# w_up of a hybrid decoder layer in three 256-column matmuls a tile, with stationary weights at bytes 64 and 192 of a line

## The chip, the cores and the metric

The kernel runs on one core of a Trainium2 chip. The metric is the device time of one execution in microseconds (us). TensorE (PE) does the matmuls; its weight loads (PEld) are instructions of their own. VectorE (DVE), ScalarE (ACT) and GpSimd (POOL) do the rest, and SyncE (SP) issues most transfers.

## The reference

One layer, 256 tokens, width 2048, all float32: an RMS norm, one input projection, sliding-window attention beside a Mamba-2 state-space part, an output projection, and then the part that the change is about, a feed-forward network with a causal convolution over three tokens:

```python
def _conv_ffn(hn, w_up, ffn_conv_w, ffn_conv_b, w_down):
    u = _causal_dwconv(hn @ w_up, ffn_conv_w, ffn_conv_b)
    gate, val = u[..., :D_FF], u[..., D_FF:]
    return (jax.nn.silu(gate) * val) @ w_down
```

D_FF is 5632, so w_up is 2048 x 11264 and w_down 5632 x 2048.

## The kernel before, in words

Every matmul operand is split in two float32r parts, `hi` (a rounded copy, made by ScalarE) and `lo` (the rest, a VectorE subtraction). A product a x b is taken as hi x hi + hi x lo + lo x hi, accumulated in PSUM. Weights come from HBM in blocks of 1 MB (512 input rows x 512 columns, as 128 partitions x 2048) into a tile `raw` (three buffers), and `pieces` and `split` (lines 75 to 101) turn each half into a `hi` and a `lo` tile of 128 x 1024 (four buffers each).

There are two kinds of product. `gemm_tok` (line 186) keeps the activations stationary and streams 512 columns of weights; it serves the q, z, k, v, w_out and (by its own loop) w_down parts. `gemm_chan` (line 212) keeps a 128 x 128 piece of the weights stationary and streams the activations of all 256 tokens, so that its output has channels on partitions, as the convolutions want it. It serves two places:

- the x, B and C channels of the state-space part: eight calls, two in each of four stretches, with `wide=False`. A tile (one 128-row block of input by 128 output channels) takes three matmuls of 256 columns: lines 229 (`hi` with the activations' `hi`), 230 (`hi` with their `lo`) and 231 (`lo` with their `hi`).
- w_up: 22 calls with `wide=True`. A tile takes two matmuls. Since the two parts of the activations of one block lie one behind the other, line 237 streams both, 512 columns, past `hi` into a whole PSUM bank; line 235 streams the 256 of `hi` past `lo` into the bank's first half. `conv` (line 243) then adds the halves, with a copy on ScalarE (line 247) and an add on VectorE (line 248), before it applies the norm's factor (249) and the taps (252, 254).

A call goes through 4 blocks x 4 output tiles x 4 input rows of 128: 64 tiles. Calls for the gate half write the four PSUM banks `acc`, those for the value half the four banks `aux`, in turn.

Where tiles begin in SBUF is set by hand. Weight and activation tiles are aligned to a line of 256 bytes, and an offset in bytes is added: `W_AT` = 0 for the weights of `gemm_tok` and of w_up, `C_AT` = 64 for those of the x/B/C calls, `X_AT` = 0 for the activations of all parts but w_up, and `H_AT` = 32 for w_up's (`h2T`). All pieces inside a tile are multiples of 256 bytes, so each matmul's operand keeps its tile's offset.

The order on each engine is made when the kernel is built, by a scheduler that models times. Small jobs (transposes, attention, state-space steps) are put between the matmuls of a large product by `later` and `step` (lines 176 to 184); in w_up only the first call has any: eight transposes (line 159) and four matmuls that spread the norm's factor (line 141).

Of the kernel before, what the change touches and what calls it, by code (L numbers as in the profile page):

```python
# [11 lines left out]
F32R = mybir.dt.float32r  # L12
I32 = mybir.dt.int32
AF = mybir.ActivationFunctionType
ALU = mybir.AluOpType
# [4 lines left out]
P = 128  # L20
D = 2048
S = 256
NT = S // P
NKT = D // P
# [14 lines left out]
HALF = 1024  # L39
LINE = 256  # L40

W_AT, C_AT, X_AT, H_AT = 0, 64, 0, 32

PAR_MIX, PAR_ATT, PAR_SSD, PAR_FFN = 0, 16, 32, 48
PAR_CW, PAR_CB = 64, 192
# [7 lines left out]
def hymba(ctx, tc, x, xt, w_kd, w_in, w_out, w_up, w_down, par, vecs, gfin, con, out):  # L53
# [20 lines left out]

    def split(raw, o, n, at):
        hi, lo = (
            wp.tile([P, HALF + C_AT // 4], F32R, tag=t, name=t, bufs=4, align_bytes=LINE)[:, at // 4 : at // 4 + n]
            for t in ("hi", "lo")
        )
        A.copy(out=hi, in_=raw[:, o : o + n])  # L80
        V.tensor_tensor(out=lo, in0=raw[:, o : o + n], in1=hi.bitcast(F32), op=ALU.subtract)  # L81
        return hi, lo

    def pieces(src, width, parts, load=None, work=None, at=W_AT):

        n = width // parts
        per = RAWW // n
        raws = [wp.tile([P, RAWW], F32, tag="raw", name="raw", bufs=3) for _ in range(-(-parts // per))]
        part = lambda h: raws[h // per][:, h % per * n : (h % per + 1) * n]
        if load:  # L90
            for h in range(parts):
                load(h)
                SY.dma_start(out=part(h), in_=src[:, h * n : (h + 1) * n])
        else:
            SY.dma_start(out=raws[0][:, :width], in_=src)
        out = []
        for h in range(parts):
            if work:
                work(h)
            out.append(split(part(h), 0, n, at))  # L100
        return out

    def acts(pool, at, **kw):
        return placed(pool, NKT * 2 * S, at, **kw).rearrange("p (k i s) -> p k i s", i=2, s=S)
# [10 lines left out]
    def col(base, i):  # L115
        c = base + i
        return parn_t[:, c : c + 1] if c < NNORM else parc_t[:, c - NNORM : c - NNORM + 1]
# [49 lines left out]
    def mm3(o, lh, ll, rh, rl, first, last):  # L167
        PE.matmul(out=o, lhsT=lh, rhs=rh, start=first, stop=False)  # L168
        PE.matmul(out=o, lhsT=lh, rhs=rl, start=False, stop=False)  # L169
        PE.matmul(out=o, lhsT=ll, rhs=rh, start=False, stop=last)  # L170
# [38 lines left out]
                if i < nb - 1 or m < 3:  # L209
                    step()  # L210

    def gemm_chan(blocks, actT, evac, tag="acc", wide=True):

        b = [acc(tag) for _ in range(4)]
        nb = len(blocks)
        for i, src in enumerate(blocks):
            got = pieces(src, 2048, 2, at=W_AT if wide else C_AT)
            last = i == nb - 1
            for ks in [(0, 1, 2, 3)] if last else [(0, 1), (2, 3)]:
                for ct in range(4):  # L220
                    for k in ks:
                        hi, lo = got[k // 2]
                        kt = 4 * i + k
                        o = (k % 2) * 512 + ct * P
                        end = kt == NKT - 1
                        rh = actT[:, kt, 0, :]
                        wh, wl = hi[:, o : o + P], lo[:, o : o + P]
                        if not wide:
                            PE.matmul(out=b[ct][:, :S], lhsT=wh, rhs=rh, start=kt == 0, stop=False)  # L229
                            PE.matmul(out=b[ct][:, :S], lhsT=wh, rhs=actT[:, kt, 1, :], start=False, stop=False)  # L230
                            PE.matmul(out=b[ct][:, :S], lhsT=wl, rhs=rh, start=False, stop=end)  # L231
                            continue
                        for lo_turn in (True, False) if end else (False, True):
                            if lo_turn:
                                PE.matmul(out=b[ct][:, :S], lhsT=wl, rhs=rh, start=False, stop=False)  # L235
                            else:
                                PE.matmul(out=b[ct], lhsT=wh, rhs=actT[:, kt, :, :], start=kt == 0, stop=end)  # L237
                    if last:
                        evac(ct, b[ct])
                    if (ct < 3) if last else (ct % 2):  # L240
                        step()

    def conv(dst, b, rB, wcol, bias, taps, wide):

        u = up.tile([P, S], F32, tag="cu", name="cu", bufs=3)
        if wide:
            A.copy(out=u, in_=b[:, S:])
            V.tensor_tensor(out=u, in0=b[:, :S], in1=u, op=ALU.add)
            V.tensor_tensor(out=u, in0=u, in1=rB, op=ALU.mult)
        else:  # L250
            V.tensor_tensor(out=u, in0=b[:, :S], in1=rB, op=ALU.mult)
        A.activation(out=dst, in_=u, func=AF.Identity, scale=wcol(taps - 1), bias=bias)
        for j in range(1, taps):
            V.scalar_tensor_tensor(  # L254
                out=dst[:, j:], in0=u[:, : S - j], scalar=wcol(taps - 1 - j), in1=dst[:, j:],
                op0=ALU.mult, op1=ALU.add,
            )
# [517 lines left out]
    for zi in range(4):  # L775
        es, parts, zt = {}, {}, {}

        def z_load(zi=zi, zt=zt):
            zt[0] = sp.tile([P, NT, 512], F32, tag="zs", name="zs", bufs=1)
            G.dma_start(out=zt[0].rearrange("p t d -> p (t d)"), in_=z_d[zi])  # L780

        def decay_loads(zi=zi, es=es):
            for g in (2 * zi, 2 * zi + 1):
                es[g] = decay_load(g)

        for g in (2 * zi, 2 * zi + 1):
            u = up.tile([P, 4, S], F32, tag="u", name="u", bufs=2)

            def evac_u(ct, b, u=u, g=g, zt=zt):
                cidx = 2 * g + ct if ct < 2 else (16 + g if ct == 2 else 24 + g)  # L790
                conv(u[:, ct, :], b, r1B, lambda k: col(PAR_CW + 32 * k, cidx), col(PAR_CB, cidx), 4, False)
                A.activation(out=u[:, ct, :], in_=u[:, ct, :], func=AF.Silu)
                if g % 2 and ct == 3:
                    A.activation(out=zt[0], in_=zt[0], func=AF.Silu)

            def part(i, g=g, u=u, es=es, parts=parts):
                if i == 0:
                    parts[g] = ssd(g, es, u)
                parts[g][i]()

            gemm_chan([w_in[5 + 3 * zi + g % 2, i] for i in range(4)], xT, evac_u, wide=False)
            if g % 2 == 0:
                later((1 if zi else 11, decay_loads), (4 if zi else 14, z_load))
            later(*(
                (off, f) for off, f in zip(
                    (5, 7, 11, 13) if g % 2 else (4, 6, 10, 12) if zi else (13, 14, 18, 20),
                    (
                        lambda g=g, es=es: decay(g, es[g]), lambda part=part: part(0),
                        lambda part=part: part(1), lambda part=part: part(2),
                    ),  # L810
                )
            ))

        def gates(zi=zi, parts=parts, zt=zt):
            for g in (2 * zi, 2 * zi + 1):
                parts[g][3](zt[0])

        gemm_att(zi)
        later(
            (1, gates), (7, lambda zi=zi, parts=parts: parts[2 * zi][4]()),  # L820
            (9, lambda zi=zi, parts=parts: parts[2 * zi + 1][4]()), *(((10, open_hp),) if zi == 3 else ()),
        )

    h2T = acts(cp, H_AT, tag="xT", name="h2T")
    ss2 = cp.tile([P, NT, 4], F32, name="ss2")
    s2 = cp.tile([P, NT], F32, name="s2")
    r2 = cp.tile([P, NT], F32, name="r2")
# [25 lines left out]
    for c in range(11):  # L853
        gate = up.tile([P, 4, S], F32, tag="u", name="gate", bufs=2)

        def evac_f(ct, b, val, c=c, gate=gate):
            i = 4 * c + ct
            ci = i + (NFT if val else 0)
            if val:
                dst = fp.tile([P, S], F32, tag="cv", name="cv", bufs=3)  # L860
            else:
                dst = gate[:, ct, :]
            conv(dst, b, r2B, lambda k: col(PAR_FW + 88 * k, ci), col(PAR_FB, ci), 3, True)
            if val:
                G.tensor_tensor(out=gT[:, i, :], in0=gate[:, ct, :], in1=dst, op=ALU.mult)  # L865
            else:
                A.activation(out=dst, in_=dst, func=AF.Silu)

        for val in range(2):
            gemm_chan(  # L870
                [w_up[2 * c + val, i] for i in range(4)], h2T, lambda ct, b, val=val: evac_f(ct, b, val),
                tag="aux" if val else "acc",
            )
# [164 lines left out]
```

## Time and profile before

| | |
|---|---|
| median of three runs | 1402.37 us (1401.41 to 1402.73) |
| profiled execution | 1398.48 us, span 1396.8 |
| PE busy | 1379.1 us, 99% of the span |
| DVE, ACT, POOL busy | 985.3, 796.0, 174.8 us |
| mean granted TensorE clock | 0.997 of full speed |
| moved by DMA | 271.76 MB, 195 GB/s |

The span is the profiled execution from the first to the last instruction. A matmul's printed duration includes a modelled end that lies beside the next matmul; when matmuls follow each other closely, the distance from start to start is what one costs. Some matmul records can be missing, so distances are taken over several rows. Times in the timeline are counted from the start of the span. By stage: the q, k, v and z parts with attention up to 258.8 us, the x/B/C stretches alternating with parts of w_out from there to 567, the rest of w_out to 657.8, w_up to 1148.2, w_down to 1387.3, and the final norm.

### The profile page before, as it was taken

To read this page: it belongs to the slowest core of one execution; us is meant where nothing else is said; L and a number is where in the kernel's file an instruction comes from. 1 tells how busy PE (TensorE), PEld (TensorE's weight loads), DVE (VectorE), ACT (ScalarE), POOL (GpSimd) and SP (SyncE) were. 2 spreads that over 40 slices of the span, in tenths; PEclk is the share of its full clock that TensorE was granted. 3 is DMA by queue.
4 is the path that set the end of the run, shared out by engine and by line. 5 is a ranking of instruction groups with operands and counts; after the bars stand their busy time and mean duration, and the time that the engine had idled before them with its cause. 6 is when DMAs were issued, how large, how long until landed. Compare 5 with 4: busy or idle time off the path is not lost.

```text
span 1396.8 us, 20383 instructions
## 1 busy us (share of the span) xinstructions
PE 1379.1 (99%) x7797; PEld 1209.5 (87%) x7797; DVE 985.3 (71%) x1488; ACT 796.0 (57%) x1275; POOL 174.8 (13%) x162
## 2 busy tenths in 40 slices
PE   8999999999999999999999999999999999999997
PEld 8888888998989899888888888888888888888886
DVE  6668788888777777655686867777687775555555
ACT  6567777775656564544564555546555554444444
POOL 0002112223111212100011101110011100000001
PEclk9999999999999999999999999999999999999999
DMA  9754544556556464656555555555555555555552
GB/s 306 263 182 166 196 151 172 190 182 209 209 187 240 170 238 169 239 185 220 191 188 184 189 201 182 181 198 179 196 193 199 181 181 209 182 200 192 187 204 91
DMA packets 44594, 271.76 MB, mean 195 GB/s; under 512 B 5056, under 2 KB 7232, under 8 KB 14672
## 3 DMA queue, kind: packets, MB, share of 16 engines
q1 hardware_dynamic: 40288, 254.69, 51.3%
q0 software_dynamic: 4208, 15.76, 3.7%
q8 instruction: 61, 1.00, 0.3%
q14 instruction: 37, 0.30, 0.1%
HBM read 264.11 MB, written 6.32 MB: 194 GB/s over the span
## 4 chain that ended last, share of the span: by engine, by line
PE 90%; DVE 3%; DMA 2%; ACT 2%; issue 1%; POOL 0%; SPq 0%; DVEq 0%; POOLq 0%; ACTq 0%
PE acc L237 11%; PE aux L237 11%; PE acc L168 11%; PE acc L170 11%; PE acc L169 11%; PE aux L235 6%; PE acc L235 6%; PE acc L231 3%; PE acc L230 3%; PE acc L229 3%; PE aux L169 3%; PE aux L170 3%; PE aux L168 3%; DVE lo L81 1%; PE aux L686 1%
## 5 line engine op out<-in xcount | busy, mean ns | idle before, releaser
L81 DVE TENSOR_TENSOR lo<-raw,hi 128x1024 fp32r<-128x1024 f32 (+1 forms) x480 | 586.3, 1229 | 328.3 <-ACT hi L80 326.7
L80 ACT CAST hi<-raw 128x1024 fp32r<-128x1024 f32 (+1 forms) x480 | 491.8, 1033 | 403.3 <-PE aux L170 126.6
L237 PE MATMUL acc<-h2T,hi 128*128 128x512 f32 x704 | 243.4, 391 | 0.0
L237 PE MATMUL aux<-h2T,hi 128*128 128x512 f32 x704 | 243.0, 391 | 0.0
L235 PE MATMUL aux<-h2T,lo 128*128 128x256 f32 x704 | 191.1, 282 | 0.0
L235 PE MATMUL acc<-h2T,lo 128*128 128x256 f32 x704 | 191.0, 282 | 0.0
L237 PEld LDWEIGHTS aux<-h2T,hi 128*128 128x128 f32 x704 | 129.8, 188 | 24.6
L237 PEld LDWEIGHTS acc<-h2T,hi 128*128 128x128 f32 x704 | 129.8, 188 | 24.5
L229 PE MATMUL acc<-xT,hi 128*128 128x256 f32 x512 | 143.8, 283 | 0.0
L230 PE MATMUL acc<-xT,hi 128*128 128x256 f32 x512 | 143.5, 282 | 0.0
L231 PE MATMUL acc<-xT,lo 128*128 128x256 f32 x512 | 141.5, 280 | 1.9 <-DVE lo L81 1.9
L235 PEld LDWEIGHTS acc<-h2T,lo 128*128 128x128 f32 x704 | 132.9, 189 | 3.9
L235 PEld LDWEIGHTS aux<-h2T,lo 128*128 128x128 f32 x704 | 132.9, 189 | 3.8
L168 PE MATMUL acc<-hi,xT 128*128 128x512 f32 (+2 forms) x320 | 113.9, 375 | 5.9 <-ACT hi L80 5.9
L170 PE MATMUL acc<-hi,xT 128*128 128x512 f32 (+2 forms) x320 | 118.6, 374 | 0.0
L169 PE MATMUL acc<-lo,xT 128*128 128x512 f32 (+2 forms) x320 | 118.5, 374 | 0.0
L865 POOL TENSOR_TENSOR gT<-gate,cv 128x256 f32<-128x256 f32 x44 | 61.1, 1390 | 434.6 <-DVE cv L254 424.1
L231 PEld LDWEIGHTS acc<-xT,lo 128*128 128x128 f32 x512 | 96.5, 190 | 2.5 <-DVE lo L81 2.1
L230 PEld LDWEIGHTS acc<-xT,hi 128*128 128x128 f32 x512 | 97.1, 190 | 0.6
L229 PEld LDWEIGHTS acc<-xT,hi 128*128 128x128 f32 x512 | 96.5, 189 | 0.3
L168 PEld LDWEIGHTS acc<-hi,xT 128*128 128x128 f32 x320 | 59.3, 191 | 15.0 <-ACT hi L80 5.9
L169 PEld LDWEIGHTS acc<-lo,xT 128*128 128x128 f32 x320 | 61.1, 191 | 9.2
(225 smaller groups left out, 2278.0 us busy)
## 6 DMA issues: line engine op xcount, KB each, us to landing
raw<-in_w_up SPq DMA_DIRECT2D x88, 1024.0 KB, 4.8
raw<-in_w_in SPq DMA_DIRECT2D x68, 1024.0 KB, 4.8
raw<-in_w_down SPq DMA_DIRECT2D x44, 1024.0 KB, 4.8
raw<-in_w_out SPq DMA_DIRECT2D x32, 1024.0 KB, 4.9
raw<-in_w_kd SPq DMA_DIRECT2D x16, 272.0 KB, 4.9
e<-acs_d POOLq DMA_DIRECT2D x8, 512.0 KB, 6.6
xraw<-in_xt SPq DMA_DIRECT2D x16, 128.0 KB, 4.4
x_r<-in_x SPq DMA_DIRECT2D x2, 1024.0 KB, 6.0
```

The source lines that it names most:

```text
L80: A.copy(out=hi, in_=raw[:, o : o + n])
L81: V.tensor_tensor(out=lo, in0=raw[:, o : o + n], in1=hi.bitcast(F32), op=ALU.subtract)
L168: PE.matmul(out=o, lhsT=lh, rhs=rh, start=first, stop=False)
L169: PE.matmul(out=o, lhsT=lh, rhs=rl, start=False, stop=False)
L170: PE.matmul(out=o, lhsT=ll, rhs=rh, start=False, stop=last)
L229: PE.matmul(out=b[ct][:, :S], lhsT=wh, rhs=rh, start=kt == 0, stop=False)
L230: PE.matmul(out=b[ct][:, :S], lhsT=wh, rhs=actT[:, kt, 1, :], start=False, stop=False)
L231: PE.matmul(out=b[ct][:, :S], lhsT=wl, rhs=rh, start=False, stop=end)
L235: PE.matmul(out=b[ct][:, :S], lhsT=wl, rhs=rh, start=False, stop=False)
L237: PE.matmul(out=b[ct], lhsT=wh, rhs=actT[:, kt, :, :], start=kt == 0, stop=end)
L686: PE.matmul(out=b[:, o : o + HD], lhsT=e[:, c, h, :], rhs=xc[:, c, h, :], start=True, stop=True)
L865: G.tensor_tensor(out=gT[:, i, :], in0=gate[:, ct, :], in1=dst, op=ALU.mult)
```

## The change

w_up loses its own form: `gemm_chan` has one path, the three 256-column matmuls of `mm3`, for both of its places, and `conv` loses the copy and the add of the wide form. `split` takes one offset for `hi` and one for `lo`: weights of `gemm_tok` and w_down stay at 0, those of `gemm_chan` now lie at 64 (`hi`) and 192 (`lo`). `h2T` goes from offset 32 to 0. For the x/B/C calls the one difference is that `lo` lies at 192 and not at 64.

```diff
-W_AT, C_AT, X_AT, H_AT = 0, 64, 0, 32
+W_AT, C_AT, X_AT = (0, 0), (64, 192), 0
...
         hi, lo = (
-            wp.tile([P, HALF + C_AT // 4], F32R, tag=t, name=t, bufs=4, align_bytes=LINE)[:, at // 4 : at // 4 + n]
-            for t in ("hi", "lo")
+            wp.tile([P, HALF + most // 4], F32R, tag=t, name=t, bufs=4, align_bytes=LINE)[:, a // 4 : a // 4 + n]
+            for t, a, most in zip(("hi", "lo"), at, C_AT)
         )
...
-            got = pieces(src, 2048, 2, at=W_AT if wide else C_AT)
+            got = pieces(src, 2048, 2, at=C_AT)
...
-                        for lo_turn in (True, False) if end else (False, True):
-                            if lo_turn:
-                                PE.matmul(out=b[ct][:, :S], lhsT=wl, rhs=rh, start=False, stop=False)
-                            else:
-                                PE.matmul(out=b[ct], lhsT=wh, rhs=actT[:, kt, :, :], start=kt == 0, stop=end)
+                        mm3(
+                            b[ct][:, :S], hi[:, o : o + P], lo[:, o : o + P], actT[:, kt, 0, :], actT[:, kt, 1, :],
+                            kt == 0, kt == NKT - 1,
+                        )
...
-        if wide:
-            A.copy(out=u, in_=b[:, S:])
-            V.tensor_tensor(out=u, in0=b[:, :S], in1=u, op=ALU.add)
-            V.tensor_tensor(out=u, in0=u, in1=rB, op=ALU.mult)
-        else:
-            V.tensor_tensor(out=u, in0=b[:, :S], in1=rB, op=ALU.mult)
+        V.tensor_tensor(out=u, in0=b[:, :S], in1=rB, op=ALU.mult)
...
-    h2T = acts(cp, H_AT, tag="xT", name="h2T")
+    h2T = acts(cp, X_AT, tag="xT", name="h2T")
```

On PE, where the last part of w_out (activations `yT`) ends and w_up (`h2T`) begins, there stands before:

```order
L168 MATMUL acc<-hi,yT 128x512
L169 MATMUL acc<-lo,yT 128x512
L170 MATMUL acc<-hi,yT 128x512
L237 MATMUL acc<-h2T,hi 128x512
L235 MATMUL acc<-h2T,lo 128x256
```

and now (the lines of `mm3` are numbered one higher):

```order
L169 MATMUL acc<-hi,yT 128x512
L170 MATMUL acc<-lo,yT 128x512
L171 MATMUL acc<-hi,yT 128x512
L169 MATMUL acc<-h2T,hi 128x256
L170 MATMUL acc<-h2T,hi 128x256
L171 MATMUL acc<-h2T,lo 128x256
```

Up to this place every engine has the same instructions in the same order in both kernels; from here on two matmuls a tile have become three. On VectorE, at the end of the first w_up call of the value half (`aux` is the PSUM bank, `cu` the convolution's input, `cv` its output, `lo` a piece of the next weights), before:

```order
L249 TENSOR_TENSOR cu<-cu,r2B 128x256
L254 SCALAR_TENSOR_TENSOR cv<-cu,parc_t,cv 128x255
L248 TENSOR_TENSOR cu<-aux,cu 128x256
L254 SCALAR_TENSOR_TENSOR cv<-cu,parc_t,cv 128x254
L254 SCALAR_TENSOR_TENSOR cv<-cu,parc_t,cv 128x255
L249 TENSOR_TENSOR cu<-cu,r2B 128x256
L254 SCALAR_TENSOR_TENSOR cv<-cu,parc_t,cv 128x254
L81 TENSOR_TENSOR lo<-raw,hi 128x1024 x2
```

and now:

```order
L238 TENSOR_TENSOR cu<-aux,r2B 128x256 x2
L241 SCALAR_TENSOR_TENSOR cv<-cu,parc_t,cv 128x255 x2
L241 SCALAR_TENSOR_TENSOR cv<-cu,parc_t,cv 128x254
L238 TENSOR_TENSOR cu<-aux,r2B 128x256
L241 SCALAR_TENSOR_TENSOR cv<-cu,parc_t,cv 128x254
L238 TENSOR_TENSOR cu<-aux,r2B 128x256
L82 TENSOR_TENSOR lo<-raw,hi 128x1024
```

The add is gone, the multiplication reads PSUM itself, and the pieces of the next weights stand among the taps in another order.

## Rows read from the trace of the kernel before

**Rows 1.** The page: busy us (share of span) and count; granted clock in 40 slices.

```profile
PE 1379.1 (99%) x7797; PEld 1209.5 (87%) x7797; DVE 985.3 (71%) x1488; ACT 796.0 (57%) x1275; POOL 174.8 (13%) x162
...
PEclk9999999999999999999999999999999999999999
```

**Rows 2.** Windows by stage: us; PE, PEld, DVE, ACT, POOL busy (count); clock, DMA.

```profile
258.85:314.45 55.60, 53.74 (x438) 53.00 (x437) 49.44 (x95) 42.21 (x83) 12.99 (x13) 0.97 0.57 190
343.32:392.11 48.79, 48.79 (x423) 48.68 (x421) 38.11 (x64) 29.73 (x43) 9.33 (x10) 1.00 0.66 238
...
491.82:541.39 49.57, 49.43 (x425) 49.10 (x423) 36.87 (x67) 29.36 (x45) 11.32 (x11) 1.00 0.61 213
...
657.78:1148.15 490.37, 490.37 (x2829) 433.50 (x2828) 361.86 (x533) 271.73 (x404) 57.67 (x42) 1.00 0.54 191
1148.15:1387.30 239.15, 239.15 (x1057) 198.01 (x1055) 129.40 (x146) 108.13 (x143) 9.26 (x9) 1.00 0.50 178
```

**Rows 3.** Groups by line, w_up on PE: busy us, mean ns, idle before.

```profile
L237 PE MATMUL acc<-h2T,hi 128*128 128x512 f32 x704 | 243.4, 391 | 0.0
...
L235 PE MATMUL acc<-h2T,lo 128*128 128x256 f32 x704 | 191.0, 282 | 0.0
```

**Rows 4.** Timeline of PE, one w_up call: start us, us, what.

```profile
703.62 0.40 PE L237 MATMUL acc<-h2T,hi 128*128 128x512 f32 x1
703.85 0.28 PE L235 MATMUL acc<-h2T,lo 128*128 128x256 f32 x1
...
725.85 0.40 PE L237 MATMUL aux<-h2T,hi 128*128 128x512 f32 x1
```

**Rows 5.** Timeline of PE, second x/B/C stretch, middle part.

```profile
353.21 0.60 PE L159 MATMUL aux<-con_t,y 128*128 128x128 f32 x4
...
365.01 0.28 PE L229 MATMUL acc<-xT,hi 128*128 128x256 f32 x1
...
366.03 0.28 PE L229 MATMUL acc<-xT,hi 128*128 128x256 f32 x1
...
381.80 0.59 PE L676 MATMUL aux<-xw,b 128*128 128x256 f32 x2
```

**Rows 6.** Timeline of PE, the same stretch, its beginning and end.

```profile
343.09 0.39 PE L170 MATMUL acc<-hi,attT 128*128 128x512 f32 x1
343.32 0.28 PE L229 MATMUL acc<-xT,hi 128*128 128x256 f32 x1
...
344.02 0.28 PE L229 MATMUL acc<-xT,hi 128*128 128x256 f32 x1
...
382.46 0.28 PE L229 MATMUL acc<-xT,hi 128*128 128x256 f32 x1
...
383.52 0.28 PE L229 MATMUL acc<-xT,hi 128*128 128x256 f32 x1
...
391.99 0.28 PE L231 MATMUL acc<-xT,lo 128*128 128x256 f32 x1
```

**Rows 7.** Waits: us, times, longest; the last row from 258 to 310, others w_up.

```profile
DVE lo L81 <- ACT hi L80: 119.0, 89, 2.6
ACT hi L80 <- PE acc L237: 83.2, 59, 3.3
...
PE acc L231 <- DVE lo L81: 1.9, 1, 1.9
```

**Rows 8.** Timeline of PE, the last job of another kind in w_up.

```profile
671.64 0.38 PE L141 MATMUL aux<-diag,ones 128*128 128x128 f32 x2
```

**Rows 9.** Groups by line: what `conv` and the split of the weights take.

```profile
L81 DVE TENSOR_TENSOR lo<-raw,hi 128x1024 fp32r<-128x1024 f32 x464 | 574.7, 1246 | 324.3 <-ACT hi L80 323.0
L80 ACT CAST hi<-raw 128x1024 fp32r<-128x1024 f32 x464 | 481.5, 1047 | 399.2 <-PE aux L170 126.6 <-PE acc L237 83.2 <-PE acc L170 80.0
...
L248 DVE TENSOR_TENSOR cu<-acc,cu 128x256 f32<-128x256 f32 x44 | 18.6, 422 | 4.1 <-ACT cu L247 4.0
...
L247 ACT COPY cu<-aux 128x256 f32<-128x256 f32 x44 | 16.4, 372 | 20.8 <-PE aux L237 20.8
```

More of the change, by code (lines that the diff above doesn't have):

```diff
@@ L210, in gemm_tok, with gemm_chan @@
                     step()
-    def gemm_chan(blocks, actT, evac, tag="acc", wide=True):
+    def gemm_chan(blocks, actT, evac, tag="acc"):
         b = [acc(tag) for _ in range(4)]
@@ L224, in gemm_chan @@
                         o = (k % 2) * 512 + ct * P
[L225 to L232, printed above, removed]
-                        for lo_turn in (True, False) if end else (False, True):
-                            if lo_turn:
-                                PE.matmul(out=b[ct][:, :S], lhsT=wl, rhs=rh, start=False, stop=False)
-                            else:
-                                PE.matmul(out=b[ct], lhsT=wh, rhs=actT[:, kt, :, :], start=kt == 0, stop=end)
+                        mm3(
+                            b[ct][:, :S], hi[:, o : o + P], lo[:, o : o + P], actT[:, kt, 0, :], actT[:, kt, 1, :],
+                            kt == 0, kt == NKT - 1,
+                        )
                     if last:
@@ L241, in gemm_chan, with conv @@
                         step()
-    def conv(dst, b, rB, wcol, bias, taps, wide):
+    def conv(dst, b, rB, wcol, bias, taps):
         u = up.tile([P, S], F32, tag="cu", name="cu", bufs=3)
-        if wide:
-            A.copy(out=u, in_=b[:, S:])
-            V.tensor_tensor(out=u, in0=b[:, :S], in1=u, op=ALU.add)
-            V.tensor_tensor(out=u, in0=u, in1=rB, op=ALU.mult)
-        else:
-            V.tensor_tensor(out=u, in0=b[:, :S], in1=rB, op=ALU.mult)
+        V.tensor_tensor(out=u, in0=b[:, :S], in1=rB, op=ALU.mult)
         A.activation(out=dst, in_=u, func=AF.Identity, scale=wcol(taps - 1), bias=bias)
@@ L790, in evac_u @@
                 cidx = 2 * g + ct if ct < 2 else (16 + g if ct == 2 else 24 + g)
-                conv(u[:, ct, :], b, r1B, lambda k: col(PAR_CW + 32 * k, cidx), col(PAR_CB, cidx), 4, False)
+                conv(u[:, ct, :], b, r1B, lambda k: col(PAR_CW + 32 * k, cidx), col(PAR_CB, cidx), 4)
                 A.activation(out=u[:, ct, :], in_=u[:, ct, :], func=AF.Silu)
@@ L799, in part @@
                 parts[g][i]()
-            gemm_chan([w_in[5 + 3 * zi + g % 2, i] for i in range(4)], xT, evac_u, wide=False)
+            gemm_chan([w_in[5 + 3 * zi + g % 2, i] for i in range(4)], xT, evac_u)
             if g % 2 == 0:
@@ L862, in evac_f @@
                 dst = gate[:, ct, :]
-            conv(dst, b, r2B, lambda k: col(PAR_FW + 88 * k, ci), col(PAR_FB, ci), 3, True)
+            conv(dst, b, r2B, lambda k: col(PAR_FW + 88 * k, ci), col(PAR_FB, ci), 3)
             if val:
```

## The prediction

> **What bounds the kernel now.** I read the page's busy times and clock first. [...] Next, the table by stage: the w_up stage lasts 490.37 us with PE busy throughout, and the four x/B/C stretches (blocks of w_in that are already done in 256-column matmuls) last 48.8 to 55.6 us each, some 203 us together, of which PE idles about 2 [rows 2]. The groups by line say that the w_up matmuls have no idle time before them [rows 3]. The waits in that stretch name only engines behind PE: ScalarE waits for PE to release a `hi` buffer, VectorE for ScalarE [rows 7]. Supply of weights is thus not the limit; if PE goes faster, the converters have room (DVE 361.86 and ACT 271.73 of 490.37 us) [rows 2].
>
> Last, the timeline, because a matmul's printed duration (391 and 282 ns) is modelled past its hand-over and adds up to more than the wall time. Only start-to-start distances count. In w_up a tile's 512-column matmul holds the array 0.23 us; one whole product (16 input blocks by 4 output tiles, 64 pairs) goes from 703.62 to 725.85, 22.23 us, so 347.3 ns a pair, which leaves 0.12 us for the 256-column one [rows 4].
>
> **What three 256-column matmuls cost.** The x/B/C stretches are the same code that w_up gets: `hi` times `hi`, `hi` times `lo`, `lo` times `hi`, with stationary pieces at byte 64 of a line and activations at 0. The timeline shows two paces there, each held for microseconds:
>
> - a quick one, 365.01 to 366.03 for three triples, 340 ns a triple [rows 5];
> - a slow one, 382.46 to 383.52 for three, 353.3 ns [rows 6].
>
> The pace is left over from what ran before. A stretch that follows 512-column matmuls starts at the slow pace (343.32, two triples in 0.70 us) [rows 6]; four 128-column transposes at 353.21 turn it quick and it is still quick at 365; a 256-column job at 381.80 (line 676) turns it slow until the stretch ends at 391.99 [rows 5, 6]. No other engine's work decides it, since both paces last through many ScalarE and VectorE instructions. A 512-column slot at its best is 239.15 us over 1057 matmuls, 226.3 ns, in w_down [rows 2]; two quick 256-column slots take 226.7, so splitting one in two costs nothing by itself, under 1 ns.
>
> **The change, part by part.**
>
> 1. w_up: 22 products of 64 tiles, 1408 pairs become 1408 triples; the array sees the same 768 columns a tile. At the quick pace a product is 64 x 340 = 21.76 us against 22.23, and 22 of them give -10.3 us. At the slow pace it is 64 x 353.3 = 22.61, +0.38 each, +8.4 us. These are the two ends for the pace, and w_up has hardly anything that could switch it: after the last odd matmul at 671.64 (line 141) [rows 8], only w_up matmuls run until 1148.15. That last job is a pair of 128-column matmuls, of the kind after which the triples came out quick at 353.21 [rows 5]. I take the quick end, as the row that it is nearest to.
>
> 2. `lo` moves from byte 64 to byte 192. No row has a stationary piece there. Its cost is bounded by the same two paces: in the x/B/C stretches all 512 triples quick, or all slow. In the stretch from 343.32 the slow parts are 343.32 to 353.21 and 382.46 to 391.99, 19.4 us of 48.79 [rows 5, 6]: at 117.8 ns a slot that is 165 slots, each 4.4 ns over the quick one, 0.73 us. Four stretches: -2.9 us if none is slow. If all were slow, the other 29 us of each hold about 250 slots, +1.1 us each, +4.4 us. I take half of the gain, -1.5 us: `hi` and `lo` at different places leave a repeating pattern less chance to hold, but nothing shows that it ends. Part of the first stretch's gain would be swallowed by a wait of 1.9 us for a `lo` piece [rows 7], whose VectorE queue does not get earlier.
>
> [...]
>
> 3. `conv` in w_up loses a ScalarE copy (372 ns, 88 of them: 32.7 us) and a VectorE add (422 ns, 88: 37.1 us) [rows 9]. Both engines wait for PE there, so this is worth 0 on the path. If that cover went, it could only be because PE waited for weights, which gets less likely with 37 us less on VectorE. It also frees the PSUM bank 0.8 us earlier, for which nobody waits, since the next product uses the other four banks.
>
> 4. h2T moves from byte 32 to 0 and w_up's weights from 0 to 64. This is the placement of the x/B/C stretches and has no cost besides the pace in 1. Transfers are the same in number and size: 0.54 of the DMA share at 22.23 us a product becomes 0.55 at 21.76 [rows 2].
>
> Sum: -10.3 - 1.5 = -11.8 us. The profiled execution took 1398.48 us (span 1396.8 and 1.7 around it), 3.9 us under the median of the three timed runs; the sum is a difference, and I take it off the median 1402.37: 1390.6 us.
>
> **Rivals.**
>
> - *The slow pace locks in over w_up.* One mechanism: the pace that TensorE has when the last odd matmul at 671.64 has gone is kept for 476 us. For it: every pace in the trace outlasts its cause, w_up is entered from 512-column matmuls, which always gave the slow pace, and nothing switches it afterwards. Against it: the transposes and line 141 stand in between. It decides as soon as more than about half of the slots are slow. Price +8.4 us, 1410.8; with the x/B/C stretches slow as well, 1415.2.
> - *A mixed pace.* The load of the `lo` piece lies 128 bytes off from the two `hi` loads, so one of three slots may be slow and two quick (344.4 ns, 22.04 us a product, -4.1 us: 1398.3), or two slow and one quick (348.9 ns, +2.2 us: 1404.6). Nothing in the trace shows a pattern of this kind inside a triple; all three slots share a pace.
> - *The places do nothing at all*, and w_up simply shows the pace of its entry. Then it is the forecast without the 1.5 us, 1392.1, or the rival above; it is no separate time, but it would make edit 2 idle.
> - *Weights come late.* A quicker w_up needs 8 pieces in 21.76 us; 8 conversions of 1.05 us on ScalarE and 8 of 1.25 on VectorE leave half of either free, `conv` aside [rows 9]. Little chance, some 2 us: 1393.
> - *Each matmul start costs a fixed time*, and there is one more a tile. The rows give under 1 ns for it, so at most +1.4 us, beside the pace. [...]
>
> **How the numbers follow.** What a measurement of this kernel can tell from no change is about 0.2%, 2.8 us. Chances: forecast and its near variants (1387 to 1394) 0.58; one slow slot of three 0.07; near no change (half of the time at either pace, two slow slots of three) 0.08; slow pace locked in, or a fixed cost, 0.27. So faster 0.65, same 0.08, slower 0.27. The forecast's own range is 1388 to 1394. To leave out no more than 2 in 10 the range has to take in the locked slow pace: 1387.5 to 1411.
>
> **What would show it.** In the changed profile: w_up products of 21.76 us from the first `acc` to the first `aux` matmul, triples of 340 ns, no PE idle in w_up, DVE there lower by some 37 us and ACT by 33. In the x/B/C stretches: whether the matmuls right after the w_out part still start at 353 ns. Products of 22.6 us make the prediction wrong by the first rival, 22.0 or 22.3 by the second. A PE wait for `lo` or `hi` in w_up would mean that the supply is the limit after all.

## The result and the profile after

The changed kernel takes 1387.69 us (median of 4, 1386.87 to 1388.62) against 1401.89 for the kernel before beside it (1400.09 to 1402.73): a ratio of 0.9901, 95% interval 0.9883 to 0.9918, or 14.2 us less. The two profiled executions lie closer, 1398.48 and 1388.62 us. In 37 further runs beside the experiments below the kernel before took 1397.04 to 1404.6 us, with medians of 1398.86 (17 runs), 1399.23 (12) and 1399.1 (7), and 1398.25 in a single one; against the three medians the changed kernel is 11.2 to 11.5 us quicker. So up to 3 us of the first difference is that spread; the profiles account for 9.9 us.

The stages of the changed kernel, as windows (columns as in [rows 2]): three of the x/B/C stretches, w_up and w_down. The last window ends two matmuls early; from its first to its last start w_down takes 239.2 us in both kernels.

```profile
259.58:314.01 54.43, 52.21 (x438) 51.17 (x437) 48.41 (x93) 40.60 (x81) 12.39 (x12) 1.00 0.55 188
344.42:392.74 48.32, 48.32 (x423) 48.22 (x421) 37.61 (x64) 29.64 (x43) 9.35 (x10) 1.00 0.66 235
...
492.38:541.90 49.52, 48.99 (x425) 48.66 (x423) 36.70 (x67) 29.17 (x45) 11.43 (x11) 1.00 0.63 213
...
658.29:1138.47 480.18, 480.18 (x4237) 480.18 (x4236) 332.59 (x448) 246.84 (x317) 51.80 (x43) 1.00 0.57 196
1138.47:1377.20 238.73, 238.73 (x1056) 197.73 (x1055) 127.91 (x141) 107.70 (x142) 7.97 (x8) 1.00 0.52 178
```

w_up went from 490.37 to 480.18 us, -10.2: that is the whole difference of the profiles. The four stretches fell only by 1.8 us together (203.4 to 201.6), and 1.5 of it came back in the w_out part after the first (28.87 to 30.41).

Of the 1.8 us, 1.2 lie in the first stretch (55.60 to 54.43), and they go with the granted clock, not with the places: it was 0.97 there before [rows 2] and is 1.00 now. After PE had waited 1.9 us for a `lo` piece, its triples in the kernel before took 643 ns for some 3 us, at a granted clock of 0.50 (307.6 to 310.9 us); in the changed kernel PE waited 2.2 us at this place and the clock stayed at 1.00 (306 to 312 us). The kernel before:

```profile
307.20 0.39 PE L231 MATMUL acc<-xT,lo 128*128 128x256 f32 x1 [1.86 <-DVE lo L81]
...
307.95 0.41 PE L229 MATMUL acc<-xT,hi 128*128 128x256 f32 x1
...
309.88 0.41 PE L229 MATMUL acc<-xT,hi 128*128 128x256 f32 x1
```

The profiles of e4, e11 and e12 below have the same 0.97 in this stretch, the others 1.00. Without that fall the first stretch takes 53.9 to 54.1 us with both parts at 64 (e2, e3, e5) and 54.0 to 54.4 with 64 and 192 (after, e1, e6, e7). With the w_out part after it, the first stretch takes 84.2 to 84.8 us in the profiles before, after and of e1 to e7. The three later stretches fell by 0.6 us (147.8 to 147.2). VectorE and ScalarE are busy 29 and 25 us less in w_up, not 37 and 33: on VectorE, a tap of the value half (128x254) went from 475 to 704 ns, for a reason that was not tried.

One w_up product on the timeline of PE, from the first `acc` to the first `aux` matmul, beside [rows 4]:

```profile
703.27 0.28 PE L169 MATMUL acc<-h2T,hi 128*128 128x256 f32 x1
703.38 0.28 PE L170 MATMUL acc<-h2T,hi 128*128 128x256 f32 x1
703.50 0.28 PE L171 MATMUL acc<-h2T,lo 128*128 128x256 f32 x1
...
725.03 0.28 PE L169 MATMUL aux<-h2T,hi 128*128 128x256 f32 x1
```

It takes 21.76 us, 340 ns a triple, as do all 21 products after the first. The group of line 171 shows no idle time before these matmuls (busy us, mean ns, idle), as [rows 3] did for the two of before:

```profile
L171 PE MATMUL acc<-h2T,lo 128*128 128x256 f32 x704 | 194.4, 276 | 0.0
```

The second x/B/C stretch, which began slow and stayed so for 10 us in [rows 6], now begins like this:

```profile
344.42 0.28 PE L169 MATMUL acc<-xT,hi 128*128 128x256 f32 x1
...
345.12 0.28 PE L169 MATMUL acc<-xT,hi 128*128 128x256 f32 x1
...
345.46 0.28 PE L169 MATMUL acc<-xT,hi 128*128 128x256 f32 x1
...
346.48 0.28 PE L169 MATMUL acc<-xT,hi 128*128 128x256 f32 x1
```

The first two triples take 0.70 us together, and the next four 1.36 us, 340 ns each. The slow pace still appears after every other job, but ends within two or three triples. Calling a gap of 116 to 130 ns between neighbouring matmuls of the triples slow, at most 8 slow gaps follow each other in the whole trace; before, up to 83 did in the stretches. The four stretches have 196 slow gaps, before 608; at 4.4 ns each that would be -1.8 us.

Why so little of that shows: PE's waits from the first stretch to the w_out part after the last (us, times, longest), beside the last row of [rows 7].

```profile
PE acc L171 <- DVE lo L82: 2.2, 1, 2.2
PE aux L682 <- ACT st L666: 1.2, 1, 1.2
PE aux L160 <- DVE y L700: 0.9, 2, 0.5
PE acc L170 <- DVE lo L82: 0.5, 1, 0.5
```

Before, the sum was 2.2 us; now it is 4.8. Not all of that comes from the place: the waits for `st` (1.0 us) and for `lo` at line 170 (0.5 us) stand also in e2 below, with both parts at 64. The wait of the transposes (line 160) for VectorE's `y` does go with it: 0.8 to 1.0 us in all five profiles with 64 and 192 (after, e1, e4, e6, e7), none in the four with 64 and 64 (before, e2, e3, e5). It falls in the third and the fourth stretch, which gained under 0.1 us each; the second has no such wait and gained 0.5 (48.79 to 48.32), what its slow gaps were worth (153, now 38). From the first x/B/C matmul to w_up the four profiles with 64 and 64 take 398.8 to 399.3 us, the five with 64 and 192 397.9 to 398.8; the means differ by 0.4 us.

### The profile page after: what moved, and what is told of

Its sections match the earlier page's. It is cut to its first block, busy times and chain, and to the rows that moved or that the text cites. A ratio compares the mean times of both kernels' runs of the same rounds, so it can differ in the third digit from the quotient of the medians.

```text
span 1386.9 us, 23003 instructions
## 1 busy us (share of the span) xinstructions
PE 1366.4 (99%) x9205; PEld 1252.8 (90%) x9205; DVE 954.6 (69%) x1400; ACT 770.6 (56%) x1187; POOL 168.3 (12%) x162
## 4 chain that ended last, share of the span: by engine, by line
PE 90%; DMA 4%; DVE 3%; ACT 1%; issue 1%; POOL 0%; SPq 0%; DVEq 0%; POOLq 0%; ACTq 0%
PE acc L169 20%; PE acc L171 20%; PE acc L170 20%; PE aux L170 9%; PE aux L171 9%; PE aux L169 9%; DMA xraw<-in_xt 1%; DMA e<-acs_d 1%; DMA h_d<-ht 1%; PE aux L673 1%; DVE u L241 1%; DVE lo L82 1%; PE aux L450 1%; PE aux L160 1%; DMA raw<-in_w_in 1%
## 5 line engine op out<-in xcount | busy, mean ns | idle before, releaser
L169 PE MATMUL acc<-h2T,hi 128*128 128x256 f32 x704 | 194.6, 276 | 0.0
L171 PE MATMUL acc<-h2T,lo 128*128 128x256 f32 x704 | 194.4, 276 | 0.0
L170 PE MATMUL acc<-h2T,hi 128*128 128x256 f32 x704 | 194.3, 276 | 0.0
L171 PE MATMUL aux<-h2T,lo 128*128 128x256 f32 x704 | 194.3, 276 | 0.0
L169 PE MATMUL aux<-h2T,hi 128*128 128x256 f32 x704 | 194.3, 276 | 0.0
L170 PE MATMUL aux<-h2T,hi 128*128 128x256 f32 x704 | 194.3, 276 | 0.0
L170 PEld LDWEIGHTS acc<-h2T,hi 128*128 128x128 f32 x704 | 132.2, 188 | 0.0
L169 PEld LDWEIGHTS acc<-h2T,hi 128*128 128x128 f32 x704 | 132.2, 188 | 0.0
L169 PEld LDWEIGHTS aux<-h2T,hi 128*128 128x128 f32 x704 | 132.2, 188 | 0.0
L170 PEld LDWEIGHTS aux<-h2T,hi 128*128 128x128 f32 x704 | 132.2, 188 | 0.0
L852 POOL TENSOR_TENSOR gT<-gate,cv 128x256 f32<-128x256 f32 x44 | 54.1, 1229 | 429.7 <-DVE cv L241 429.7
```

## The experiments

Theory A: with `hi` and `lo` at one place (64), TensorE holds whichever of the two paces the job before left; with 64 and 192 it comes back to the quick one. Rival B: the places do nothing.

**e1: the place alone.** The kernel before, with `lo` at 192 in the x/B/C calls.

```diff
-W_AT, C_AT, X_AT, H_AT = 0, 64, 0, 32
+W_AT, C_AT, X_AT, H_AT = (0, 0), (64, 192), 0, 32
...
```

Expected: 

> The kernel before with one edit: in the x/B/C calls lo lies at byte 192 instead of 64; w_up keeps its two matmuls a tile and its places. Theory A (the two places end the slow pace after a few matmuls): no run of 117 to 119 ns slots longer than a dozen in the four x/B/C stretches, their sum 203.4 us falls by 1 to 3 us, w_up stays at 22.23 us a product, the whole time 1 to 3 us lower. Rival B (the places do nothing, the pace is only what the job before left): stretches still begin at 353 ns a triple after 512-column matmuls and stay so, no change of the time.

Measured: 1400.48 us, ratio 1.0002 (0.9989 to 1.0015): no change. The stretches sum to 201.1 us, 2.3 less than before, 1.6 of it in the first, where the clock had been lower before; w_up stays at 22.23 us a product. In the stretches the pace did as A says, with at most 8 slow gaps in a row; the time did as B says. PE's waits in this run have the same three causes as those of the changed kernel:

```profile
PE acc L231 <- DVE lo L81: 1.8, 1, 1.8
PE aux L695 <- ACT st L679: 1.0, 1, 1.0
PE aux L159 <- DVE y L713: 0.8, 2, 0.5
```

**e2: three matmuls, both parts at 64.** The changed kernel with

```diff
-W_AT, C_AT, X_AT = (0, 0), (64, 192), 0
+W_AT, C_AT, X_AT = (0, 0), (64, 64), 0
```

Expected: 

> The changed kernel with one edit: lo at byte 64 like hi, in w_up too. Theory A: whichever pace the last odd job (line 142) leaves is held through w_up. After the like jobs at 353 us of the kernel before it was the quick one, so 21.76 us a product and a time within 3 us of the changed kernel (the x/B/C stretches slow in part again, as before); if it leaves the slow one, 22.61 us a product, 18 us more than the changed kernel. Rival B expects the same as A here. A third theory C (places at 64 and 64 are slow in themselves whenever nothing shakes them) expects 22.61 us.

Measured: 1387.91 us, ratio 0.9918 (0.9898 to 0.9937) to the kernel before, as quick as the changed one. On PE's timeline w_up starts slow after the w_out part (47 slow gaps in a row), and turns quick after the first two matmuls of line 142:

```profile
656.08 0.39 PE L171 MATMUL acc<-hi,yT 128*128 128x512 f32 x1
656.30 0.28 PE L169 MATMUL acc<-h2T,hi 128*128 128x256 f32 x1
...
656.66 0.28 PE L169 MATMUL acc<-h2T,hi 128*128 128x256 f32 x1
...
665.66 0.38 PE L142 MATMUL aux<-diag,ones 128*128 128x128 f32 x2
...
666.24 0.28 PE L169 MATMUL acc<-h2T,hi 128*128 128x256 f32 x1
...
667.26 0.28 PE L169 MATMUL acc<-h2T,hi 128*128 128x256 f32 x1
...
701.50 0.28 PE L169 MATMUL acc<-h2T,hi 128*128 128x256 f32 x1
...
723.26 0.28 PE L169 MATMUL aux<-h2T,hi 128*128 128x256 f32 x1
```

The three triples from 666.24 take 340 ns each, and a product 21.76 us. Between the first triples and line 142 stand the eight transposes of line 160, of 128 columns like those at 353.21 in [rows 5]; they left the slow pace as it was, here and in e3 and e5. Theory C, that 64/64 is slow in itself, is out. For w_up, A and B are not yet told apart, since the entry was lucky. PE's waits over the same part as above:

```profile
PE acc L171 <- DVE lo L82: 1.7, 1, 1.7
PE aux L682 <- ACT st L666: 1.0, 1, 1.0
PE acc L170 <- DVE lo L82: 0.5, 1, 0.5
```

**e3 and e4: one small job more.** Both place a float32 matmul of 256 columns after line 142, e3 in the kernel of e2, e4 in the changed one.

```diff
+    def job():
+        b = aux()
+        PE.matmul(out=b[:, :S], lhsT=ones, rhs=con_t[:, 0:S], start=True, stop=True)
+        V.tensor_copy(out=warm, in_=b[:, 0:1])
+
+    later((10, job))
```

Expected of e3: 

> The kernel of e2 with one more small job in the first w_up call, after line 142: a float32 matmul of 256 columns, the form after which the x/B/C stretches of the kernel before went slow (line 676), with a one-column copy of its result that is used nowhere. Theory A: it leaves the slow pace and nothing ends it: 22.61 us a product from there to w_down, about 18 us more than the changed kernel, some 1406 us. A rival D (64/64 finds back to the quick pace by itself): 21.76 us and under 1 us more than e2.

Expected of e4: 

> The changed kernel (64 and 192) with the same added job as e3. Theory A: at most a dozen slots over 115 ns after the job, then 113.3 ns again: 21.76 us a product, time within 1 us of the changed kernel. Rival B: slow like e3, 22.61 us a product.

Measured: e3 1387.92 us, ratio 0.9921 (0.9902 to 0.994); e4 1392.21 us in its one run. Both have 21.76 us a product. e4's run had lost 3 us before the first stretch, which began at 262.67 instead of 259.58. So this job does not leave the slow pace; that line 676 did so in [rows 5] is not a rule on 256-column jobs. Inconclusive on A.

**e5 and e6: a job that does leave it.** Twelve 512-column float32r matmuls with both operands at byte 0, as in the w_out parts, after line 142; e5 with both parts at 64, e6 with 64 and 192.

```diff
+        for j in range(12):
+            PE.matmul(out=b, lhsT=h2T[:, 0, 0, 0:P], rhs=h2T[:, 0, :, :], start=j == 0, stop=j == 11)
...
```

Expected of e5: 

> The kernel of e2 (narrow, hi and lo both at 64) with another added job in the first w_up call after line 142: twelve float32r matmuls of 512 columns with both operands at byte 0, like the w_out part after which every x/B/C stretch began slow, and a one-column copy of the result that is used nowhere. Theory A (at 64/64 the pace that the job before leaves is held): the slow pace from there to w_down, 22.61 us a product, about 2.7 us for the job and 17 us for the pace over e2, some 1408 us. Rival D (in w_up 64/64 finds back to the quick pace by itself, or such a job does not set it): 21.76 us a product, about 3 us over e2, 1391 us.

Expected of e6: 

> The changed kernel (64 and 192) with the added job of e5. Theory A: about eight slots over 115 ns after the job, then 113.3 ns: 21.76 us a product, about 3 us over the changed kernel for the job itself, 1391 us. Rival B (the places do nothing): the same as e5, whatever that is.

Measured: e5 1411.0 us, ratio 1.0082 (1.0063 to 1.0102); e6 1391.97 us, ratio 0.995 (0.9931 to 0.9968). The same job, 19 us apart. PE in e5:

```profile
676.14 2.91 PE L837 MATMUL aux<-h2T 128*128 128x512 f32 x12
678.89 0.28 PE L169 MATMUL acc<-h2T,hi 128*128 128x256 f32 x1
...
709.98 0.28 PE L169 MATMUL acc<-h2T,hi 128*128 128x256 f32 x1
...
732.59 0.28 PE L169 MATMUL aux<-h2T,hi 128*128 128x256 f32 x1
```

and in e6:

```profile
673.96 2.91 PE L837 MATMUL aux<-h2T 128*128 128x512 f32 x12
676.70 0.28 PE L169 MATMUL acc<-h2T,hi 128*128 128x256 f32 x1
...
706.64 0.28 PE L169 MATMUL acc<-h2T,hi 128*128 128x256 f32 x1
...
728.40 0.28 PE L169 MATMUL aux<-h2T,hi 128*128 128x256 f32 x1
```

e5 has 22.61 us a product, and all the products that follow, until w_down at 1162.25: the slow pace, once left behind, held for 483 us without any other work on PE, at a granted clock of 1.00. e6 has 21.76. B is out.

**e7: two matmuls a tile at the new places.** The kernel before with

```diff
-W_AT, C_AT, X_AT, H_AT = 0, 64, 0, 32
+W_AT, C_AT, X_AT, H_AT = (0, 0), (64, 192), 0, 0
...
-            got = pieces(src, 2048, 2, at=W_AT if wide else C_AT)
+            got = pieces(src, 2048, 2, at=C_AT)
```

Expected: 

> The kernel before (two matmuls a tile in w_up) with the places of the changed one everywhere: hi at 64, lo at 192, activations at 0. If the gain of w_up comes from the places and not from the three matmuls (theory E), a pair goes from 347.3 to 340 ns, 21.76 us a product, and the time to that of the changed kernel. If it comes from the split into 256-column matmuls (theory F), the pair keeps 346 to 349 ns, 22.2 us a product, and the time stays within 2 us of the kernel before.

Measured: 1404.47 us, ratio 1.0035 (1.002 to 1.0049), 22.50 us a product:

```profile
706.85 0.39 PE L237 MATMUL acc<-h2T,hi 128*128 128x512 f32 x1
...
729.35 0.39 PE L237 MATMUL aux<-h2T,hi 128*128 128x512 f32 x1
```

At these places the gain needs the three matmuls; the pair is dearer here than at its old places, by 0.27 us a product. Three matmuls at w_up's old places (weights at 0, activations at 32) were not run, so whether the three alone would have gained is not shown.

**e8: everything at 0.** The changed kernel with `C_AT` = (0, 0). Expected: 

> The changed kernel with hi and lo at byte 0, where the activations lie too. If places only decide how the pace is kept (theory A), w_up runs at 340 or at 353 ns a triple, 21.76 or 22.61 us a product. If place 0 collides with the activations in itself (theory G: each matmul's columns and the next weights fall on the same part of a line), all slots are at least 117.8 ns whatever came before: 22.6 us a product or more, 18 us over the changed kernel, and the x/B/C stretches slow throughout. If places do nothing (rival B), 21.76 us and the time of the changed kernel.

Measured: 1421.88 us, ratio 1.0156 (1.0134 to 1.0179), 23.04 us a product, 360 ns a triple, in the x/B/C stretches too:

```profile
715.00 0.28 PE L169 MATMUL acc<-h2T,hi 128*128 128x256 f32 x1
...
738.04 0.28 PE L169 MATMUL aux<-h2T,hi 128*128 128x256 f32 x1
```

The place of the weights alone is worth 34 us between e8 and the changed kernel.

**e9 to e12: which of the two places does it.** The kernel of e6 with `C_AT` = (192, 192), (128, 128) and (192, 64), and for e12 the changed kernel with (192, 64) and no added job. The tile of each part is made large enough for 192.

Expected of e9: 

> The kernel of e6 (changed kernel with the twelve added 512-column matmuls, results unused) with hi and lo both at byte 192. Theory H (it is the distance of 128 bytes between hi and lo that ends the slow pace): both at one place is like 64/64 in e5, 22.61 us a product after the job. Theory I (it is lo, or anything, at 192 that ends it): 21.76 us.

Expected of e10: 

> The kernel of e6 with hi and lo both at byte 128. Theory H: one place for both, so a pace that is held: 22.61 us a product, or like 0/0 (23.04 us) if half a line from the activations collides as the same place does. Theory I: not 192, so not 21.76 us after the job.

Expected of e11: 

> The kernel of e6 with the two places exchanged: hi at 192, lo at 64. Theory H: still 128 bytes apart, so about eight slow slots after the job and then 21.76 us a product. Theory I in its narrow form (lo must lie at 192): held at 22.61 us.

Expected of e12: 

> The changed kernel with the two places exchanged, hi at 192 and lo at 64, and no added job. In e11 the same places kept a slow pattern of about 356 ns a triple from the transposes and through line 142, until the twelve added matmuls ended it. Theory H (128 bytes between hi and lo are enough): it ends by itself, 21.76 us a product, the time of the changed kernel. Theory J (which of the two parts lies at 192 matters, and exchanged they hold a slow pattern too): 64 x 356 = 22.8 us a product for the 21 later products, some 22 us over the changed kernel, about 1410 us.

Measured, one run each but e12: e9 1411.85 us and 22.61 us a product, slow already before the job; e10 1423.36 us and 23.04 us, as with all at 0; e11 1390.94 us and 21.76 us after the job. With e9 theory I is out: both parts lie at 192, and the slow pace stays. e10 shows that 360 ns a triple do not need the activations' own place, as theory G had it: half a line away costs the same. But e11 is no clean support for theory H: before the job it ran slow, from the transposes of line 160 on and through both pairs of line 142, in a pattern of two unlike triples:

```profile
666.06 0.28 PE L169 MATMUL acc<-h2T,hi 128*128 128x256 f32 x1
...
666.77 0.38 PE L142 MATMUL aux<-diag,ones 128*128 128x128 f32 x2
...
667.36 0.28 PE L169 MATMUL acc<-h2T,hi 128*128 128x256 f32 x1
...
672.92 2.93 PE L837 MATMUL aux<-h2T 128*128 128x512 f32 x12
```

From 666.06 the two triples to 666.77 take 0.71 us. e12, without the job that ended this, took 1413.31 us, ratio 1.0109 (1.0092 to 1.0126), with 22.82 us a product (356.6 ns a triple) up to w_down:

```profile
706.59 0.28 PE L169 MATMUL acc<-h2T,hi 128*128 128x256 f32 x1
...
729.41 0.28 PE L169 MATMUL aux<-h2T,hi 128*128 128x256 f32 x1
```

Theory H is out, J stands: a distance of 128 bytes is not enough; `hi` at 64 with `lo` at 192 came back to the quick pace after every job tried, and the same places exchanged did not after line 142 (e12). Why the places act in this way is not shown by any run.

## Why the prediction was right, and where it was not

- *w_up at the quick pace, -10.3 us*: measured -10.2 in the profiles, 21.76 us a product as worked out. The reason given, that the last odd job of line 142 (141 before) leaves the quick pace, is what e2 shows for 64/64. With 64 and 192 it was not needed: e6 ends quick from the opposite entry, so in the changed kernel the pace comes back by itself, of which the working said that nothing shows it. The step from the transposes at 353.21 to line 141 was lucky, too: in e2 jobs of that shape left the slow pace, and only line 142 ended it.
- *The slow pace locks in*: the rival's mechanism and price were right for another placement. e5 took 1411.0 us with 22.61 us a product; the rival said 22.61 and 1410.8. That the totals agree so well is chance: e5 holds an added job of 2.75 us, and the kernel before took 1399.23 us beside it, not the 1402.37 of the forecast. In the changed kernel it did not happen after any of the jobs tried here.
- *`lo` at 192, -1.5 us in the x/B/C stretches*: the term of the sum that was mis-sized. The pace did more than half of what was allowed (412 fewer slow gaps, -1.8 us), but from the first x/B/C matmul to w_up the profiles show only -0.4 us between the means of the two placements, and e1's time is unchanged. The working had looked for one swallowed wait in the first stretch, where indeed nothing was gained, and not at what the jobs between the triples wait for: the two waits for `y` in the later stretches took back 0.9 us. It also passed over the granted clock of 0.97 in the first stretch [rows 2], which the 40 slices of the page, a 9 each, do not show [rows 1].
- *A mixed pace within the triple*: "all three slots share a pace" was taken from 64/64 alone. e11 and e12 have slots of 117, 118 and 125 ns in one pattern. For the places of the change it did not come about.
- *A 256-column job turns it slow*: true of line 676 (353.3 ns a triple after it [rows 6]), not of e3's job (340). Which property of a job decides was not settled; the form in the profile is the same for both, two records of 128x256.
- *The places do nothing at all*: no. The same instructions take 340 ns a triple at 64/192 and 360 at 0/0 (e8). What makes the difference is not shown.
- *Each matmul start costs a fixed time*: no. Two slots of 256 columns take 226.7 ns in w_up's quick triples, and one of 512 in w_down 226.7 from start to start (1056 matmuls). The working's 226.3 divides the stage by 1057, where its bounds, the first and the last start, hold 1055 distances.
- *Weights come late, `conv`, the transfers*: no wait of PE in w_up, as worked out, and a product is 64 triples of 340 ns, which leaves no gain for `conv`.

The total was -14.2 us in the first comparison where -11.8 was forecast, and 11.2 to 11.5 against the later runs of the kernel before. The profiles show -9.9; the other 4 us lie in no stage of the profiles, and the spread of the kernel before is the likeliest place, though not shown to be. Part of that spread stands ahead of the x/B/C stretches: the first began at 257.43 us in e2, 258.85 before and 262.87 in e1, with the same instructions up to there. What makes that part vary was not tried.

## What to carry to other kernels

When PE is busy throughout, read its pace from start to start over many instructions and compare stretches of the same code: two paces there at an unchanged granted clock, here 340 and 353 ns a triple at 1.00, are a sign that something other than the columns sets it. Where each 128 x 128 piece of float32r weights serves only 256 columns, as here, try the byte places of the weight tiles, each part by itself, and test them from a bad entry, since a placement that only happens to start well (e2, 1387.91 us) looks the same as one that recovers (1387.69). A quicker stretch gains less if the small jobs woven into it are then late, as here by 0.9 us of waits for `y`: look for what they wait for before counting the gain. And before two single profiles are compared stage by stage, compare the granted clock of the stage: here 1.2 us of a gain were a clock that fell in one of them.

## What the runs showed of the hardware that was not expected

With 128 x 128 float32r weights, 256 columns and activations at byte 0 of a line (places as `hi`/`lo`): 0/0 and 128/128 gave 360 ns a triple, 192/192 gave 353, 64/64 held 353 or 340 depending on what ran before, 192/64 held 356.6 or 340, and 64/192 always came back to 340 within about eight matmuls. The 353 of e5 held for 483 us and the 340 of the changed kernel for 457 us (21 products), both at a granted clock of 1.00, so these two paces are not the clock's; the profiled runs with 360 (e8, e10) and 356.6 (e12) had a mean clock of 0.995 to 0.997 over the whole span, too near full speed for a w_up 5 or 6% longer. A 512-column matmul in w_down, with both operands at byte 0, takes 226.7 ns in the profiles of before, after, e2, e5 and e8, as long as two of 256 columns at the quick pace.
